# Five edits at the seams of a two-layer hybrid block: rounded-form norm products, an earlier first gather, ln2 folded into x^T, and an alternating split

## The chip, the cores and the metric

The kernel runs on one core of a Trainium2 chip, as one program. The metric is the time of one execution on the device in microseconds. TensorE (PE) multiplies matrices, VectorE (DVE), ScalarE (ACT) and GpSimd (POOL) do the elementwise work, SyncE (SP) starts most of the transfers.

## The reference, cut to what matters

Two layers over 512 tokens of width 1024. Each layer projects x, mixes the tokens in three ways (sparse attention, a gated delta net, a convolution), projects back, normalises, sends each token to 2 of 32 experts, and normalises again.

```python
for l in range(DEPTH):
    h = x @ w_in[l]
    ...
    y_gdn = _gated_deltanet(gdn_qkv, gdn_z, gdn_b, gdn_a, ...)   # q and k are l2-normalised
    mix = jnp.concatenate([y_nsa, y_gdn, y_conf], axis=-1) @ w_out[l]
    x = _layer_norm(DEEPNORM_ALPHA * x + mix, ln1_w[l], ln1_b[l])
    moe = _hier_moe(x, w_group, b_group, w_expert, b_expert, w_gate, w_up, w_down)
    x = _layer_norm(DEEPNORM_ALPHA * x + moe, ln2_w[l], ln2_b[l])
```

All is float32; the products must keep more digits than one rounded-form (F32R) product has.

## The kernel before

Tokens lie in four tiles of 128 (`xr[t]`, t = 0 to 3). TensorE has two ways to multiply float32 here: a full fp32 product, which the trace shows as two records, and the faster product of tiles declared F32R, which holds rounded operands. Where precision matters a value is split into hi (rounded) and lo (the rest), and the products hi·hi, hi·lo and lo·hi are summed (`mm3`, L355 to L357).

A layer goes through these stages. The in-projection transposes x (`xT_ps`, L318), splits it (`xTh`, `xTl`), splits pieces of the weights (`w_hl`, hi by ACT L350, lo by DVE or POOL L351) and fills the PSUM banks `ipA` and `ipB`. In between, the generator `delta_net` and the attention are woven in. `delta_net` makes three rows of inverse norms per head for all tokens (`g_rs`), transposes them (`g_rsT`, L507), and spreads them over the 64 channels of a head by products with a 0/1 selector (`hsel` in the constants; `g_rsb`, L514), six products of a layer; DVE multiplies the six results into q and k. The compression (`cmp_h`) is fp32 too. Then come the out-projection (`opA`, `opB`, `wo_hi`, `wo_lo`), the first normalisation with the router, and the sort of the 32 experts by their load (`r_swp`, `r_sorted`, `r_srt`).

The experts run in nine cycles, largest last ranks sorted into fixed slots of 192 to 32 tokens. SP's queue streams every expert's 6 MB (`w_gu`, `w_d`) through a ring of 13 slots. For a cycle `m_oh` marks which token stands in which slot, `m_ix` are its products, `m_tok` and `m_idx` the token numbers, and POOL gathers the tokens from a DRAM copy of the normalised x (`x1D`) into `xg`; `m_g` transposes, `m_xe` applies the first normalisation's weights, `f_gu` and `f_y` are the two products of the expert, `f_h` the activation, `f_hT` and `f_hTs` its transpose. `y_split` writes an expert's result as hi and lo (`m_yh` by ACT, `m_yl` by DVE); `m_sc` scatters these and DVE adds them to `xr`. The last cycle's results are added in `m_fin`: an fp32 product of `xr` with the identity and four products of `m_yh` and `m_yl` for each tile; statistics, ACT's scale and shift, then `ln_w` and `ln_b` by DVE or POOL follow.

The engines' instruction orders come from a list scheduler at build time; TensorE's order in the expert stage is the program's own (a manual schedule). The lines that a sentence can't say well, the selector product and the split:

```python
T.matmul(ps, C("hsel")[32 * i:32 * i + 4, b * P:(b + 1) * P], rsT[32 * i:32 * i + 4, :],
         start=True, stop=True)
...
for n in range(nj):
    A.copy(hi[:, n * nw:(n + 1) * nw], src[n])
for n in range(nj):
    V.tensor_tensor(lo[:, n * nw:(n + 1) * nw], src[n], hi[:, n * nw:(n + 1) * nw].bitcast(F32), op=ALU.subtract)
```

Of the kernel before, what the change touches and what calls it, by code (L numbers as in the profile page):

```python
# [112 lines left out]
def hybrid_kernel(ctx, tc, x_in, w_in, w_out, cmp_pe, cmp_w1, cmp_w2, conv_w, a_log, dt_bias, norm_w,  # L113
                  dw_w, dw_b, cln_w, cln_b, ln1_w, ln1_b, ln2_w, ln2_b, w_grp, b_grp, w_exp, b_exp,
                  w_gate, w_up, w_down, consts, out, R=3, R2=9, R4=1, NG=10, NE=9, WL=6, layers=DEPTH, CN=32, GI=2, CV0=5, CV1=30, CVM="A", EB=12, SC="GAGA", LB2="GGVVVVVV", TO="0123", HL=3, LOP=4, LOM="10110101", XP=6, ORDER="GkGcomGqPwfx0yG1t2z3GGr"):
# [189 lines left out]
    for l in range(layers):  # L305
        if l:
            mixer, kat, delta, psum = open_mixer(l)

        phase = open_pool(f"inp{l}", "inp")
        xTh, xTl = [], []  # L310
        for kp in range(4):
            a = tp("inp", "xT", 8, f"xTh{kp}", F32R)
            b = tp("inp", "xT", 8, f"xTl{kp}", F32R)
            for kk in range(2):
                k = 2 * kp + kk
                ps = bank("xT_ps")
                for t in range(NT):
# [1333 lines left out]
```

## Time and profile before

| | us |
|---|---|
| timed runs: median of 3 (lowest, highest) | 1934.66 (1930.06, 1935.19) |
| profiled execution | 1942.38 |
| its span in the trace | 1940.6 |
| PE busy in it | 1726.5 (89%) |
| DVE, ACT, POOL busy | 1010.8, 573.2, 390.0 |

The profile is one execution, some 8 us above the median. Its rows give durations and waits; the timed runs give what two kernels are compared by. "Idle before" stands behind an instruction with the event that ended the idle time. The granted clock is TensorE's, 1.00 for its higher level of 2.4 GHz and 0.50 for 1.2 GHz, a mean where a window holds both.

### The profile page before, as it was taken

The page shows a single profiled execution, that of the slowest core. Times are in us where ns is not written, and L with a number is a line of the kernel's source. Part 1 is how long each engine was busy: PE and PEld are TensorE (multiplying, and loading weights), DVE is VectorE, ACT ScalarE, POOL GpSimd, SP SyncE. Part 2 cuts the span into 40 slices and gives each one's busy share as a digit, 9 for nine tenths or more (in the row PEclk, how much of TensorE's full clock was granted, in tenths as well). Part 3 has the DMA queues.
Part 4 walks back from the last instruction along what each step waited for, and adds up shares of the span by engine and source line. Part 5 has one row for each costly group of instructions (what it writes and reads, how often), then busy time and mean ns, then how long its engine had stood idle before and what let it go on. Part 6 is the DMA issues. An engine that isn't in the chain of part 4 may idle for free. (4 is left out here: it accounts for less than half of the span.)

```text
span 1940.6 us, 31342 instructions
## 1 busy us (share of the span) xinstructions
PE 1726.5 (89%) x11812; PEld 1013.2 (52%) x11812; DVE 1010.8 (52%) x2258; ACT 573.2 (30%) x1250; POOL 390.0 (20%) x354
## 2 busy tenths in 40 slices
PE   7899699979889899999789987999698898999996
PEld 6776576763443434333377775767534444343343
DVE  2756877464432524343627678765742334343345
ACT  3342565422210112111234336554221111121122
POOL 2234641324000000000123366323140000000001
PEclk9998699989999899999989975999799998999997
DMA  5221000388999979999632310005799999799994
GB/s 181 88 87 66 1 2 23 130 337 341 408 400 404 404 297 394 409 362 409 250 109 76 99 44 1 13 12 188 285 397 408 403 404 404 282 410 408 363 409 154
DMA packets 147339, 478.41 MB, mean 247 GB/s; under 512 B 23032, under 2 KB 25584, under 8 KB 147184
## 3 DMA queue, kind: packets, MB, share of 16 engines
q1 hardware_dynamic: 138304, 456.74, 61.2%
q10 hardware_dynamic: 4144, 10.70, 1.6%
q0 software_dynamic: 4736, 8.92, 1.3%
q8 instruction: 95, 1.56, 0.3%
q14 instruction: 60, 0.49, 0.1%
HBM read 476.04 MB, written 8.39 MB: 250 GB/s over the span
## 5 line engine op out<-in xcount | busy, mean ns | idle before, releaser
L1291 PE MATMUL f_gu<-w_gu,m_xe 128*32 128x256 f32 (+1 forms) x3456 | 398.0, 453 | 27.4 <-DMA w_gu<-in_moe_w_up 23.2
L1291 PEld LDWEIGHTS f_gu<-w_gu,m_xe 128*32 128x32 f32 (+1 forms) x3456 | 134.7, 118 | 277.8 <-issue 227.7
L1323 PE MATMUL f_y<-w_d,f_hTs 128*32 128x256 f32 (+2 forms) x1824 | 253.0, 474 | 9.3 <-ACT f_hTs L1308 2.9
L1333 DVE TENSOR_TENSOR m_yl<-f_y,m_yh 32x256 fp32r<-32x256 f32 (+2 forms) x222 | 115.3, 520 | 257.9 <-ACT m_yh L1331 250.2
L1383 POOL DMA_INDIRECT xg<-x1D,m_idx x34 | 36.1, 1063 | 753.2 <-PE f_hT L1306 331.9
L1331 ACT CAST m_yh<-f_y 32x256 fp32r<-32x256 f32 (+2 forms) x222 | 98.4, 443 | 299.5 <-PE f_y L1323 297.2
L1444 DVE TENSOR_TENSOR xr<-xr,m_sc 128x1024 f32<-128x1024 f32 x128 | 153.1, 1219 | 26.6 <-PE m_sc L1443 25.4
L1323 PEld LDWEIGHTS f_y<-w_d,f_hTs 128*32 128x32 f32 (+2 forms) x1824 | 82.5, 124 | 157.8 <-issue 127.0
L1298 DVE SCALAR_TENSOR_TENSOR f_h<-f_h,m_wsl,f_gu 128x128 f32<-128x128 f32 (+1 forms) x76 | 33.0, 434 | 229.1 <-ACT f_h L1297 228.7
L1297 ACT ACTIVATE f_h<-f_gu 128x128 f32<-128x128 f32 (+1 forms) x76 | 26.4, 348 | 392.4 <-PE f_gu L1291 298.6
L1443 PE MATMUL m_sc<-m_yh,m_ohT 128*128 128x512 f32 (+1 forms) x256 | 115.4, 451 | 28.9 <-DVE xr L1444 28.6
L351 POOL TENSOR_TENSOR w_hl<-w_slice,w_hl 128x512 fp32r<-128x512 f32 (+1 forms) x54 | 71.9, 1334 | 229.9 <-ACT w_hl L350 220.8
L1443 PE MATMUL m_sc<-m_yl,m_ohT 128*128 128x512 f32 (+1 forms) x256 | 104.7, 409 | 0.0
L350 ACT CAST w_hl<-w_slice 128x512 fp32r<-128x512 f32 (+1 forms) x96 | 56.0, 589 | 145.6 <-PE ipB L357 117.2
L1287 PE MATMUL f_gu<-w_gu,m_xe 128*128 128x512 f32 x192 | 89.1, 610 | 0.4 <-DMA w_gu<-in_moe_w_gate 0.3
L1443 PEld LDWEIGHTS m_sc<-m_yh,m_ohT 128*128 128x128 f32 (+1 forms) x256 | 50.1, 196 | 65.7 <-DVE xr L1444 43.4
L766 POOL TENSOR_TENSOR cvt<-cvt,cv_t 128x485 f32<-128x485 f32 (+28 forms) x66 | 78.3, 1187 | 17.9 <-ACT cv_t L762 16.2
L1028 ACT ACTIVATE e<-a_s,a_nm 128x128 f32<-128x128 f32 (+3 forms) x128 | 66.5, 527 | 44.9 <-DVE a_nm L1023 42.5
L1426 PE MATMUL m_g<-ident,xg 128*128 128x128 f32 (+2 forms) x272 | 47.7, 299 | 19.5 <-DMA xg<-x1D,m_idx 16.2
L1287 PEld LDWEIGHTS f_gu<-w_gu,m_xe 128*128 128x128 f32 x192 | 35.3, 193 | 53.2 <-issue 49.0
L1023 DVE TENSOR_REDUCE a_nm<-a_s 128x1 f32<-128x384 f32 (+3 forms) x88 | 55.3, 635 | 11.9 <-PE a_s L1020 11.0
L351 DVE TENSOR_TENSOR w_hl<-w_slice,w_hl 128x512 fp32r<-128x512 f32 (+1 forms) x42 | 29.3, 697 | 61.8 <-ACT w_hl L350 61.5
(474 smaller groups left out, 3310.0 us busy)
## 6 DMA issues: line engine op xcount, KB each, us to landing
w_gu<-in_moe_w_gate SPq DMA_DIRECT2D x256, 512.0 KB
w_gu<-in_moe_w_up SPq DMA_DIRECT2D x256, 512.0 KB
w_d<-in_moe_w_down SPq DMA_DIRECT2D x128, 1024.0 KB
w_slice<-in_w_in SPq DMA_DIRECT2D x20, 1024.0 KB
w_out<-in_w_out SPq DMA_DIRECT2D x16, 1024.0 KB
x1D<-xr SPq DMA_DIRECT2D x8, 512.0 KB
w_slice<-in_w_in SPq DMA_DIRECT2D x4, 560.0 KB
x<-in_x SPq DMA_DIRECT2D x4, 512.0 KB
```

Of the source, the lines that this page charges most:

```text
L350: A.copy(hi[:, :n], src)
L351: (G if LOE(npc[0], k) else V).tensor_tensor(lo[:, :n], src, hi[:, :n].bitcast(F32), op=ALU.subtract)
L766: G.tensor_tensor(ac2[:, 30 - j:512], ac2[:, 30 - j:512], tm, op=ALU.add)
L1023: V.tensor_reduce(nm[:, 0:hb], ps[:, :hb * L].rearrange("p (h l) -> p h l", h=hb), axis=AX.X, op=ALU.max, negate=True)
L1028: A.activation(e[:, :L], ps[:, i * L:(i + 1) * L], AF.Exp, bias=nm[:, i:i + 1], accum_out=sums[:, i0 + i:i0 + i + 1])
L1287: T.matmul(pg[:, i, :], xe(k), wv[:, i, :], start=(k == 0), stop=(k == 7), skip_group_check=True)
L1291: T.matmul(pg[j * c:(j + 1) * c, 0, 0:2 * fw], xe(k), wv[:, :, j * fw:(j + 1) * fw], start=(k == 0), stop=(k == 7), skip_group_check=True)
L1323: T.matmul(o, lt, wv[:, n * nw:(n + 1) * nw], start=(k == 0), stop=(k == 3), skip_group_check=True)
L1331: A.copy(hi[:, n * nw:(n + 1) * nw], src[n])
L1333: V.tensor_tensor(lo[:, n * nw:(n + 1) * nw], src[n], hi[:, n * nw:(n + 1) * nw].bitcast(F32), op=ALU.subtract)
L1443: T.matmul(ps2[:, n, :], ohT[0:nr, t * P:(t + 1) * P], y[0:nr, n * 512:(n + 1) * 512], start=(i == 0), stop=(i == 1))
L1444: V.tensor_tensor(xr[t][:, :D], xr[t][:, :D], ps2.rearrange("p a b -> p (a b)"), op=ALU.add)
```

## The change

Five edits. (A) The inverse norms are split into hi and lo, put side by side in eight rows, and spread by one F32R product with the selector (`hselr`) instead of an fp32 one. (B) The first cycle's slot marks, token numbers and gather are written ahead of the sort; the DRAM copies of x go by POOL's queue. (C) Between the layers the second normalisation's weights are applied to x^T (channels are rows there, so they are a scale and an offset of ACT's activation), and to the residual later, behind pieces of the in-projection; two of the four `m_fin` tiles leave out the identity product, DVE adds `xr` instead. (D) At the end of the program the scale and shift are four DVE instructions a tile. (E) In `y_split` each copy is followed by its subtract. The path for experts over their slots, not run here, becomes a function. Core of the diff:

```diff
-            V.tensor_scalar(rs3[:, :, 2, 0:4], rn[:, :, 4:8], 0.5, None, op0=ALU.mult)
...
+            rsf, rsh = rs3[:, :, :, 8:12], small("g_rsh", [P, NT, 3, 4], F32R, bufs=1, key="g")
...
+            A.copy(rsh, rsf)
+            V.tensor_tensor(rs3[:, :, :, 4:8], rsf, rsh.bitcast(F32), op=ALU.subtract)
+            V.tensor_copy(rs3[:, :, :, 0:4], rsh.bitcast(F32))
...
-            rsT = s512("g_rsTs")
+            rsT = s512("g_rsTs", F32R)
...
-                    T.matmul(ps, C("hsel")[32 * i:32 * i + 4, b * P:(b + 1) * P], rsT[32 * i:32 * i + 4, :],
+                    T.matmul(ps, hselr[32 * i:32 * i + 8, b * P:(b + 1) * P], rsT[32 * i:32 * i + 8, :],
...
-                nc.sync.dma_start(x1D[l][t * P:(t + 1) * P, :], xr[t][:, :D])
+                G.dma_start(x1D[l][t * P:(t + 1) * P, :], xr[t][:, :D])
...
+        prep_oh(0)
+        ps0 = bank("m_ix0")
+        place_mm(0, ps0, 2, tokb)
+        tokens(0, ps0, 2)
+
         key, keyc = small("r_key", [64, 32], bufs=1), small("r_keyc", [64, 1], bufs=1)
...
             for n in range(nj):
                 A.copy(hi[:, n * nw:(n + 1) * nw], src[n])
-            for n in range(nj):
                 V.tensor_tensor(lo[:, n * nw:(n + 1) * nw], src[n], hi[:, n * nw:(n + 1) * nw].bitcast(F32), op=ALU.subtract)
...
+                    w, o = scale[:, k:k + 1], scale[:, 8 + k:9 + k]
+                    A.activation(hi, ps, AF.Identity, scale=w, bias=o)
+                    xk = xa[:, kk * 512:kk * 512 + 512]
+                    V.tensor_scalar(xk, ps, w, o, op0=ALU.mult, op1=ALU.add)
+                    (G if kk else V).tensor_tensor(lo, xk, hi.bitcast(F32), op=ALU.subtract)
...
+                if later and npc[0] >= 2 and on is V:
+                    for _ in range(2):
+                        f, t = later.popleft()
+                        f(t, made)
...
+        order = (0, 1, 2, 3) if end else (2, 3, 0, 1)
...
+            add = not end and t >= 2
+            if not add:
                 for n in range(2):
+                    T.matmul(fin[t][n], ident, xr[t][:, n * 512:(n + 1) * 512], start=True, stop=False, skip_group_check=True)
+            last_results(t, fin[t], add)
+            if add:
+                V.tensor_tensor(xr[t][:, :D], xr[t][:, :D], f2.rearrange("p a b -> p (a b)"), op=ALU.add)
...
+                if end:
+                    V.scalar_tensor_tensor(o, fin[t][n], mu, lw[:, n * 512:(n + 1) * 512], op0=ALU.subtract, op1=ALU.mult)
+                    V.scalar_tensor_tensor(o, o, rs, lb[:, n * 512:(n + 1) * 512], op0=ALU.mult, op1=ALU.add)
+                else:
+                    A.activation(o, fin[t][n], AF.Identity, scale=rs, bias=nb)
...
+            xTh, xTl = x_transposed(xr, prm[l][:, 124:140])
```

Three places in the engines' orders. The first is TensorE in the in-projection of layer 0, around the transposes of the norms, before:

```order
L355 MATMUL ipB<-xTh_132,w_hl 128x512
L356 MATMUL ipB<-xTl_133,w_hl 128x512
L507 MATMUL g_rsT<-ident,g_rs_1254 96x128 x4
L357 MATMUL ipA<-xTh_132,w_hl 128x512
L355 MATMUL ipA<-xTh_132,w_hl 128x512
```

and of the change, 62 rows later in its order:

```order
L920 MATMUL cmp_h<-kk,w_cmp 128x65 x16
L914 MATMUL cmp_tr<-ident,kva_691 128x128 x2
L914 MATMUL cmp_tr<-ident,kva_692 128x128 x2
L549 MATMUL g_rsT<-ident,g_rs_1262 96x128 x4
L393 MATMUL ipA<-w_hl,xTh_117 128x512
L394 MATMUL ipA<-w_hl,xTh_117 128x512
```

`g_rsT` has moved from the middle of a row of in-projection products to the place behind the compression's transposes. The second place is VectorE after the router in layer 0 (`r_sw` the slot places, `r_key` to `r_pm` the sort of the experts, `m_oh` the slot marks), before:

```order
L1107 TENSOR_TENSOR r_sw_3528<-r_oh_4025,r_oh_4026 128x2x32
L1223 SCALAR_TENSOR_TENSOR r_key<-r_pos,cst 64x32
...
L1361 TENSOR_TENSOR m_oh<-cst,r_sw_3528 128x4x64 x2
L1227 TENSOR_REDUCE r_rank<-r_key 64x1
L1229 TENSOR_SCALAR r_pm<-cst,r_rank 64x64
L1239 COPY r_srt<-r_sorted 128x256
...
L1379 TENSOR_REDUCE m_tok<-m_ix_4202 128x1
...
L1380 TENSOR_SCALAR m_idx<-m_tok 128x1
...
L1246 TENSOR_TENSOR r_tw_4161<-r_rest,r_tw_4161 128x4x2
L1371 TENSOR_SCALAR m_xe_4200<-m_g_4214,w1c_3475,b1c_3476 128x128
```

and of the change:

```order
L1149 TENSOR_TENSOR r_sw_3540<-r_oh_4037,r_oh_4038 128x2x32
L1274 TENSOR_TENSOR m_oh<-cst,r_sw_3540 128x4x64 x2
L1319 SCALAR_TENSOR_TENSOR r_key<-r_pos,cst 64x32
...
L1284 TENSOR_REDUCE m_tok<-m_ix_4150 128x1
L1323 TENSOR_REDUCE r_rank<-r_key 64x1
L1285 TENSOR_SCALAR m_idx<-m_tok 128x1
L1325 TENSOR_SCALAR r_pm<-cst,r_rank 64x64
L1335 COPY r_srt<-r_sorted 128x256
...
L1342 TENSOR_TENSOR r_tw_4192<-r_rest,r_tw_4192 128x4x2
L1438 TENSOR_SCALAR m_xe_4148<-m_g_4226,w1c_3487,b1c_3488 128x128
```

The token numbers (`m_idx`) now stand ahead of the sort's result `r_srt`; the first `m_xe` stands at its old place, behind all of the sort's rows. The third place is ACT and VectorE at an expert of 32 rows, with the engines whose work an instruction waits for; ACT before and of the change:

```order
L1331 CAST m_yh<-f_y 32x256 [waits PE_49]
L1331 CAST m_yh<-f_y 32x256 x3
L1297 ACTIVATE f_h<-f_gu 128x128 [waits PE_49]
```

```order
L1427 CAST m_yh<-f_y 32x256 [waits PE_49]
L1427 CAST m_yh<-f_y 32x256 [waits DVE_49] x3
L1393 ACTIVATE f_h<-f_gu 128x128 [waits PE_49]
```

and VectorE before and of the change:

```order
L1333 TENSOR_TENSOR m_yl<-f_y,m_yh 32x256 [waits Activation_49]
L1333 TENSOR_TENSOR m_yl<-f_y,m_yh 32x256 x3
```

```order
L1428 TENSOR_TENSOR m_yl<-f_y,m_yh 32x256 [waits Activation_49] x4
```

Three of ACT's copies have got a wait for VectorE, and three of VectorE's subtracts one for ACT.

## Rows read from the trace of the kernel before

**Rows 1.** The page: the span and the busy table (busy us, share, instructions of each engine).

```profile
span 1940.6 us, 31342 instructions
PE 1726.5 (89%) x11812; PEld 1013.2 (52%) x11812; DVE 1010.8 (52%) x2258; ACT 573.2 (30%) x1250; POOL 390.0 (20%) x354
```

**Rows 2.** Windows of layer 0's expert stage: the busy us of each engine with its instructions, TensorE's granted clock, the DMA engines' share, and GB/s.

```profile
560.00:680.00 120.00, 102.94 (x628) 49.51 (x624) 47.50 (x108) 18.30 (x44) 4.53 (x4) 0.93 1.03 405
840.00:945.00 105.00, 101.56 (x966) 42.37 (x962) 44.84 (x91) 21.97 (x60) 2.46 (x3) 0.98 0.95 370
```

**Rows 3.** TensorE's waits over the whole program: what it waited for, us in total, times, the longest.

```profile
PE m_g L1426 <- DMA xg<-x1D,m_idx: 16.2, 6, 6.3
PE a_cmp L963 <- DVE qs L957: 11.4, 7, 2.9
```

**Rows 4.** The group of the `g_rsb` products over both layers (busy us, mean ns), and TensorE's timeline of layer 0 with start, duration, shape and count.

```profile
L514 PE MATMUL g_rsb<-g_rsTs,cst 4*128 4x512 f32 x24 | 14.5, 713 | 0.0
138.52 1.98 PE L514 MATMUL g_rsb<-g_rsTs,cst 4*128 4x512 f32 x4
145.33 0.39 PE L357 MATMUL ipA<-w_hl,xTl 128*128 128x512 f32 x1
145.56 0.40 PE L355 MATMUL ipA<-w_hl,xTh 128*128 128x512 f32 x1
149.57 5.10 PE L878 MATMUL cmp_h<-kk,w_cmp 128*128 128x65 f32 x32
154.60 3.78 PE L514 MATMUL g_rsb<-g_rsTs,cst 4*128 4x512 f32 x4
```

**Rows 5.** The group of the `g_rsT` transposes over both layers (the idle time ahead of them last).

```profile
L507 PE MATMUL g_rsT<-ident,g_rs 128*96 128x128 f32 x8 | 1.2, 276 | 3.9 <-DVE g_rs L504 3.9
```

**Rows 6.** Windows around these products, columns as in rows 2.

```profile
118.00:138.00 20.00, 18.03 (x100) 15.32 (x99) 9.73 (x14) 8.88 (x16) 6.85 (x6) 1.00 0.34 106
142.00:145.00 3.00, 3.00 (x9) 2.32 (x8) 2.90 (x6) 0.09 (x1) 0.00 (x0) 0.50 0.19 72
150.00:162.00 12.00, 12.00 (x44) 8.56 (x43) 11.79 (x25) 1.61 (x4) 0.00 (x0) 0.58 0.37 127
```

**Rows 7.** The timelines of ACT, VectorE, TensorE and POOL from the end of layer 0's router to its first expert.

```profile
416.23 2.37 ACT L1160 ACTIVATE xr<-xr,ln_rs 128x1024 f32<-128x1024 f32 x2 [0.50 <-DVE ln_rs L302]
423.61 0.29 DVE L1219 SCALAR_TENSOR_TENSOR r_sw<-r_pos,r_selb 128x128 f32<-128x128 f32 x1
424.85 0.74 DVE L1361 TENSOR_TENSOR m_oh<-cst,r_sw 128x256 bf16<-128x256 f32 x2
428.75 0.26 PE L1391 MATMUL m_ix<-tokb,m_oh 128*128 128x2 bf16 x4
431.10 1.24 POOL L1383 DMA_INDIRECT xg<-x1D,m_idx  x1 [13.91 <-DVE m_idx L1380]
432.87 0.17 DVE L1246 TENSOR_TENSOR r_tw<-r_rest,r_tw 128x8 bf16<-128x8 f32 x1
435.32 1.12 PE L1426 MATMUL m_g<-ident,xg 128*128 128x128 f32 x4 [6.32 <-DMA xg<-x1D,m_idx]
436.05 0.84 DVE L1371 TENSOR_SCALAR m_xe<-m_g,w1c,b1c 128x128 f32<-128x128 f32 x2 [3.02 <-PE m_g L1426]
436.52 1.98 PE L1291 MATMUL f_gu<-w_gu,m_xe 128*64 128x512 f32 x4
```

**Rows 8.** The timelines of ACT and VectorE in the last experts of layer 0.

```profile
859.92 2.70 ACT L1331 CAST m_yh<-f_y 64x512 fp32r<-64x512 f32 x6 [11.35 <-PE f_y L1323]
921.32 2.68 ACT L1331 CAST m_yh<-f_y 64x512 fp32r<-64x512 f32 x6 [6.21 <-PE f_y L1323]
929.41 1.50 ACT L1331 CAST m_yh<-f_y 32x256 fp32r<-32x256 f32 x4 [2.51 <-PE f_y L1323]
930.93 1.73 DVE L1333 TENSOR_TENSOR m_yl<-f_y,m_yh 32x256 fp32r<-32x256 f32 x4 [2.12 <-ACT m_yh L1331]
932.86 0.28 ACT L1297 ACTIVATE f_h<-f_gu 128x128 f32<-128x128 f32 x1 [1.96 <-PE f_gu L1291]
933.17 0.35 DVE L1298 SCALAR_TENSOR_TENSOR f_h<-f_h,m_wsl,f_gu 128x128 f32<-128x128 f32 x1 [0.51 <-ACT f_h L1297]
```

**Rows 9.** The timelines of TensorE and ACT from the end of layer 0 to the first products of layer 1.

```profile
943.18 1.93 PE L1323 MATMUL f_y<-w_d,f_hTs 128*32 128x256 f32 x32
945.18 1.50 ACT L1331 CAST m_yh<-f_y 32x256 fp32r<-32x256 f32 x4 [2.49 <-PE f_y L1323]
948.64 1.95 PE L1598 MATMUL m_fin<-xr,ident 128*128 128x512 f32 x4 [3.52 <-DVEq L1522]
955.26 1.66 ACT L350 CAST w_hl<-w_slice 128x512 fp32r<-128x512 f32 x3 [8.57 <-DMA ln_b<-in_ln_b]
972.23 1.54 PE L318 MATMUL xT_ps<-ident,xr 128*128 128x128 f32 x6 [11.39 <-ACT xr L1610]
976.57 0.80 PE L355 MATMUL ipA<-xTh,w_hl 128*128 128x512 f32 x1 [0.46 <-ACT xTh L250]
```

**Rows 10.** The DMA issues: POOL's load of `m_iot`, count, KB of each, median us from issue to landing.

```profile
m_iot<-consts POOLq DMA_DIRECT2D x2, 256.0 KB, 6.1
```

**Rows 11.** VectorE's timeline at the end of the program: the first statistics and the last add.

```profile
1916.34 1.30 DVE L296 BATCH_NORM_STATS2 ln_st<-m_fin 128x6 f32<-128x512 f32 x2 [6.00 <-PE m_fin L1603]
1935.05 1.23 DVE L1614 TENSOR_TENSOR xr<-xr,ln_b 128x1024 f32<-128x1024 f32 x1
```

More of the change, by code (lines that the diff above doesn't have):

```diff
@@ L205, in load_consts @@
         V.tensor_copy(trib, C("tri_pos"))
+        V.tensor_copy(hselr, C("hsel"))
         V.tensor_copy(tokb, C("tokc").rearrange("p (t c) -> p t c", c=2))
+    hselr = cp.tile([P, 256], F32R, name="hselr")
     tokb = cp.tile([P, NT, 2], BF16, name="tokb")
@@ L305, in hybrid_kernel, with scale_residual, offset_residual @@
     for l in range(layers):
[L306 to L317, printed above, removed]
-                    T.transpose(ps[:, t * P:(t + 1) * P], xs[t][:, k * P:(k + 1) * P], ident)
-                split(a[:, kk * 512:kk * 512 + 512], b[:, kk * 512:kk * 512 + 512], ps)
-            xTh += [a[:, 0:512], a[:, 512:1024]]
-            xTl += [b[:, 0:512], b[:, 512:1024]]
+        if l == 0:
+            xTh, xTl = x_transposed(xs)
+        def scale_residual(t, behind):
+            with tc.issue_after(behind.ins):
+                V.tensor_tensor(xr[t][:, :D], xr[t][:, :D], lw[:, :D], op=ALU.mult)
+        def offset_residual(t, behind):
+            with tc.issue_after(behind.ins):
+                V.tensor_tensor(xr[t][:, :D], xr[t][:, :D], lb[:, :D], op=ALU.add)
+            A.dma_start(x_res[t * P:(t + 1) * P, :], xr[t][:, :D])
+        later = deque((f, t) for t in range(NT) for f in (scale_residual, offset_residual)) if l else deque()
         def load_slice(cuts):
@@ L1587, in hybrid_kernel @@
-        lw, lb = t4("ln_w"), t4("ln_b")
+        overflow()
+        end = l == layers - 1
+        lw, lb = (t4("ln_w"), t4("ln_b")) if end else (x4("ln_w"), x4("ln_b"))
         row_bcast(lw[:, :D], ln2_w[l])
@@ L1611, in hybrid_kernel @@
-        for t in TO:
-            t = int(t)
-            (V if LB2[2 * t] == "V" else G).tensor_tensor(xr[t][:, :D], xr[t][:, :D], lw[:, :D], op=ALU.mult)
-            (V if LB2[2 * t + 1] == "V" else G).tensor_tensor(xr[t][:, :D], xr[t][:, :D], lb[:, :D], op=ALU.add)
-            if l == layers - 1:
+                        T.matmul(o[n], OHT[cy, u][0:nr, t * P:(t + 1) * P], y[0:nr, n * 512:(n + 1) * 512],
+                                 start=first and i == 0 and j == 0, stop=(i == 1 and j == len(last[t]) - 1), skip_group_check=True)
@@ new lines, in hybrid_kernel @@
+        fixed.close()
+        for t in order:
+            mu, rs, nb = norm_stats(fin[t])
+            for n in range(2):
+                o = xr[t][:, n * 512:(n + 1) * 512]
+                if end:
+                    V.scalar_tensor_tensor(o, fin[t][n], mu, lw[:, n * 512:(n + 1) * 512], op0=ALU.subtract, op1=ALU.mult)
+                    V.scalar_tensor_tensor(o, o, rs, lb[:, n * 512:(n + 1) * 512], op0=ALU.mult, op1=ALU.add)
+                else:
+                    A.activation(o, fin[t][n], AF.Identity, scale=rs, bias=nb)
+            if end:
@@ L1622, in hybrid_kernel @@
         close(psum)
-        xs = xr
+        if not end:
+            psum, kat, phase = open_input(l + 1)
+            xTh, xTl = x_transposed(xr, prm[l][:, 124:140])
+            moe.close()
+            mixer, delta = open_mixer(l + 1)
+        else:
+            moe.close()
 _INS = ['x', 'w_in', 'w_out', 'nsa_cmp_pe', 'nsa_cmp_w1', 'nsa_cmp_w2', 'gdn_conv_w', 'gdn_a_log', 'gdn_dt_bias',
```

299 lines of the change are left out of this document (154 added, 145 removed).

## The prediction

> **What bounds the kernel now.** I read the page's busy table and slices first [rows 1]: TensorE works 1726.5 of 1940.6 us, so an edit counts only if it shortens TensorE's own work or one of its waits. The windows show where even that fails [rows 2]: from 560 to 680 us the DMA share is 1.03 and TensorE works 102.9 of 120 us, so the weight stream sets the end there; from 840 to 945 TensorE works 101.6 of 105. The list of TensorE's waits comes next [rows 3]. Most of it lies inside the expert stage; the waits that this change can touch are those for `xg` (16.2 us, longest 6.3), for `g_rs` (3.9, two) [rows 5], and, between the layers, `m_fin`'s 3.52 and `xT_ps`'s 11.39 [rows 9].
>
> **A. The norms' products.** The six `g_rsb` products of a layer are full fp32: 24 records in the two layers, 14.5 us [rows 4]. The row of layer 0 shows four records in 1.98 us, two products, so about one us each. The F32R product of the same 128x512 output starts every 0.23 us beside it at full clock [rows 4] (145.33, then 145.56). After the change all twelve products are of that kind, with eight rows of weights in place of four: 12 x 0.23 = 2.8. Saved 14.5 - 2.8 = 11.7 us. I take the number of weight rows as free, since the 128-row F32R products have that pitch too.
>
> `g_rsT` now stands between `ipB` and `ipA`, and TensorE waits there for `g_rs`, 3.9 us in both layers [rows 5]. In the changed order it stands behind the compression's transposes, some 60 instructions later, where `g_rs` is long made; the wait goes. The additions are an ACT cast, a VectorE subtract and a copy, each of 48 elements a partition, so shorter than the 0.35 us f_h rows of 128 [rows 8]; they lie in the time that `g_rsT` has been moved by. The norms come later by some matmuls, but in the windows of rows 6 TensorE is busy nearly throughout and VectorE is not (15.3 of 20 us): the products set the pace, so I put that at nothing; if the delta net's chain were exposed, the first product's move from 138.5 to about 142 costs 3.5 us a layer, 7 in all. A = 11.7 + 3.9 = 15.6; I take 15.
>
> The clock is a bonus that I leave out of the sum. Behind the fp32 products the granted clock is 0.50 in 142 to 145 and 0.58 in 150 to 162 [rows 6]. If the rise came at once, 3.0 us of work would take 1.5, and of the 12 us, less the 3.8 of `g_rsb` already counted, some 3.4 would go: 5 us in this layer, 10 at most with the other. But the compression's fp32 products (5.10 us, 32 records at 149.57) stay, and they end in the same half-clock stretch [rows 4]. So: between 0 and 10, I take 0.
>
> **B. The moved gather.** Now the first expert's gather stands behind the sort: VectorE writes `r_sw` at 423.61, TensorE does `r_swp`, `r_sorted` and the others before `m_ix` at 428.75, POOL issues the gather at 431.10 and TensorE starts `m_g` at 435.32, after 6.32 us idle [rows 7]. After the change `m_oh` follows `r_sw` directly: 423.61 + 0.29 + 0.3 (`r_sw`'s second half) + 0.74 = 424.9, the placement products 0.3, `m_tok` and `m_idx` behind five short VectorE rows: about 426.2. The gather goes 4.9 us earlier, and with the same 4.2 us from issue to `m_g` its data lie there at 430.6. But the next VectorE row that the expert needs, `m_xe`, still stands behind the whole sort [order of VectorE, above], which ends at 432.87 + 0.17 now, and after the change about 0.7 later, since two `m_oh` (0.74) stand ahead of it. So `m_xe` starts near 433.8, takes 0.42, and `f_gu` starts at 434.3 instead of 436.52: 2.2 us a layer, 4.4 in both. Bounds: 0, if nothing moves, and 9, if `m_xe` came as early as the data. The stream passes it on: its first slot is freed by this expert.
>
> The copies of x for the gather go by POOL's queue instead of SP's. POOL can issue the last when ACT has made it, 416.23 + 2.37 = 418.6 [rows 7], about 419.5 with the others ahead. The nearest row is POOL's `m_iot`: 256 KB in 6.1 us from issue to landing [rows 10]. At that price 425.6, at twice it 431.7; the gather's index is ready at 426.2. I take it as just hidden. A rule speaks against this move: the Trainium skill's page DMA: Bandwidth & Descriptors (section SWDGE vs HWDGE vs iDMA) says that DMAs from GpSimd's queue have their descriptors written by GpSimd's cores, which VectorE can lock out of SBUF in some of its modes, and that queues of SP and ACT are immune. No run here shows such a stall. By it the copies would land late and B would be lost, which is a rival below.
>
> **C. Between the layers.** TensorE ends its last `f_y` at 945.1, waits 3.52 us for the split of `f_y`, needs 12 us for `m_fin`, and waits 11.39 for the normalised, scaled and shifted `xr`; the first `ipA` starts at 976.57 [rows 9]. The change takes the fp32 identity products out of two tiles (1.95 each in the row), puts an add of 1.23 for each on VectorE [rows 11], and moves the eight multiplies and adds of `ln_w` and `ln_b` out of the chain: they come later, under the in-projection. TensorE's `m_fin` then ends near 957. VectorE from 950: two adds and one pair of statistics, 3.7, to 954; then two `w_hl` rows, whose ACT casts start at 955.26, because ACT's queue stands 8.57 us for the landing of `ln_b` [rows 9]: to 957.7 as now. Then three pairs of statistics (1.30 each, rows 11), 3.9, and small rows, to 962.3; ACT's tiles at 1.2 each [rows 7], the last two behind the last statistics, end near 966; transposes (1.0) and the scaled cast (0.6, as `w_hl`'s) bring `ipA` to about 967.6. Gain 9. It would be 12 if the `w_hl` rows did not hold VectorE, and 5 if `ln_b`'s landing came later by the two loads that stand with it.
> The eight moved rows, 8 x 1.23 = 9.8 us, go behind VectorE's pieces in the in-projection, which TensorE bounds; uncovered, they cost up to that much.
>
> **D. The end.** The last tile's add ends at 1935.05 + 1.23 = 1936.28 and the output lands at 1940.6. After the change VectorE does a tile in 1.30 for two statistics over 512, 0.5 for small rows and 4 x 0.65 for the new ones at the same size: 4.4 us. From 1916.34 [rows 11] four tiles end at 1934.0, with two short waits for `m_fin` near 1935. Gain 1.3, between 0 and 2.
>
> **E. The split of `f_y`.** Copy and subtract now alternate, and each waits for the other engine [order of ACT and VectorE, above]. Today four copies take 1.50 us and four subtracts 1.73 behind them [rows 8]: in series already. Alternating adds seven hand-overs; one takes 0.05 (932.86 + 0.28 = 933.14, next row at 933.17). 0.35 more for each 32-row expert. It is exposed ahead of `m_fin`, twice. ACT is free for the next `f_h` by then, as it comes 3.45 us after the split's start. Where six parts of two experts run together (three times, 859.92 to 921.32) `f_h` follows them at once, 0.4 each by the same hand-overs. 2 x (0.4 + 1.2) = 3.2; I take 3. Bounds 0 and, at one us for each of the eight splits from 859.92 to 945.18 [rows 8, 9] in each layer, 16.
>
> **Sum.** 15 + 4.4 + 9 + 1.3 - 3 = 26.7. The profiled execution took 1942.4, above the three timed runs (median 1934.7); so its profile should read 1915.7, and the median 1908.
>
> **Rivals.**
> *The clock follows* (A gives 8 more): 1900. For it, the low clock stands right behind the fp32 products; against it, the compression's products stay.
> *The norms are a chain* (the delta net gives 7 of TensorE's gain back, by the bound under A): 1915. For it, TensorE's 11.4 us of waits for `qs` show chains behind the in-projection [rows 3].
> *`ln_b` holds the boundary* (C gives 5 instead of 9, since two more small loads stand in that queue): 1912. The row of 955.26 speaks for it [rows 9].
> *POOL's copies are late*: the gather stands for them until 431, B is gone: 1912.4.
> *The same mechanism, far worse*: if the copies, issued at 419.5, land beyond 444.5, the first `f_gu` slips over 13.4 us behind today's in each layer and the change is slower, 1936 or more. One step decides it, a landing 25 us after issue, four times `m_iot`'s.
> *The waits of the split are paid often* (8 late experts a layer at 0.8 us in place of 3 in all): 13 instead of 3, 1918.
>
> **Chances.** Forecast 0.47, clock 0.14, norms' chain 0.12, boundary 0.07, copies late 0.07, split 0.07, slow copies 0.03, several losses together 0.03. Range 1897 to 1924: below it lies a clock gain with more of C, above it two of the losses together. A measurement tells 0.3% (6 us) from no change; faster is 0.92, same 0.05, slower 0.03.
>
> **What would show it.** A: `g_rsb` near 0.25 us a record and no wait before `g_rsT`; the clock in 140 to 160 tells the first rival. B: POOL's gather about 5 us ahead, `f_gu` only 2 us, with `m_xe` as what is waited for; if the gather waits for a DMA, the copies are late. C: the first `ipA` about 24.5 us after the last `f_y`'s start instead of 33.4 (943.18 to 976.57). D: the add's row is gone and VectorE runs without a gap. E: the span from the first copy to `m_fin` is 3.8 us instead of 3.5. Wrong it would be if `m_fin`'s or the delta net's waits grow by what the products save.

## The result and the profile after

The changed kernel takes **1910.24 us** (median, 1907.17 to 1913.2) against 1934.93 (1930.06 to 1938.69) for the kernel before: a ratio of 0.9854, 95% interval 0.9813 to 0.9895. The forecast was 1908, the range 1897 to 1924. Two more measurements of the same kernel gave 0.9887 and 0.9839. The profiled execution took 1907.17 us with this span:

```profile
span 1905.4 us, 31305 instructions
PE 1709.5 (90%) x11794; PEld 1004.8 (53%) x11794; DVE 1021.5 (54%) x2281; ACT 569.4 (30%) x1248; POOL 390.7 (21%) x362
```

Against [rows 1] TensorE works 17.0 us less and the span is 35.2 us shorter. The span overstates the gain: the execution profiled before lay 8 us above its median, this one 3 below. To see where the time went, I cut each profile at the same marks of TensorE's timeline, both layers added (us): the in-projection from the first `ipA` to the last `ipB` or `ipA` (the norms' products lie in it); the mixers from there to the last `opB`, the output projection's last product; the routing from there to the first `f_gu`; the experts from there to the end of the last `f_y`; the boundary from there to layer 1's first `ipA`; and the tail from layer 1's last `f_y` to the end.

| kernel | in-proj. | mixers | routing | experts | routing + experts | boundary | tail | span |
|---|---|---|---|---|---|---|---|---|
| before | 327.2 | 467.5 | 51.05 | 1016.8 | 1067.9 | 31.46 | 33.6 | 1940.6 |
| norms_alone | 309.0 | 473.2 | 50.91 | 1013.0 | 1063.9 | 31.33 | 29.7 | 1919.9 |
| **after** | 309.6 | 466.8 | 46.00 | 1019.2 | 1065.2 | 23.85 | 27.4 | 1905.4 |
| after_again | 309.3 | 466.7 | 45.99 | 1022.0 | 1068.0 | 24.32 | 31.6 | 1912.9 |
| after_third | 310.3 | 469.6 | 46.00 | 1021.3 | 1067.3 | 24.69 | 30.6 | 1915.3 |
| f32r_4rows | 311.3 | 474.0 | 46.01 | 1018.6 | 1064.6 | 23.98 | 31.8 | 1918.4 |
| fp32_8rows | 320.3 | 476.3 | 46.02 | 1016.9 | 1062.9 | 23.60 | 29.5 | 1925.2 |
| x1D_sp | 311.1 | 468.3 | 46.00 | 1018.3 | 1064.3 | 24.44 | 28.9 | 1910.0 |
| xe_early | 311.1 | 466.8 | 44.21 | 1022.0 | 1066.2 | 23.96 | 29.0 | 1909.9 |
| split_undone | 310.3 | 469.2 | 46.02 | 1019.7 | 1065.7 | 21.38 | 27.2 | 1906.6 |
| ln_sp | 310.4 | 468.2 | 46.00 | 1022.0 | 1068.0 | 22.88 | 30.9 | 1913.5 |
| best | 309.5 | 472.1 | 43.51 | 1022.3 | 1065.8 | 20.84 | 31.5 | 1912.4 |
| ids_late | 309.2 | 468.1 | 46.01 | 1007.8 | 1053.8 | 24.92 | 29.1 | 1897.7 |
| ids_split | 310.5 | 474.4 | 46.00 | 1011.2 | 1057.2 | 21.31 | 28.8 | 1904.9 |

The three profiles of the unchanged new kernel show how far a column may be trusted: routing within 0.01, boundary and in-projection within 1, mixers and experts within 3, tail within some 4 us (over all rows with the same mixers, 466.7 to 474.4). So the gain stands in the in-projection (-17.6, -17.9 and -16.9), at the boundary (-6.8 to -7.6), in the tail (-2.0 to -6.2), and in the routing (-5.05). But the experts grow by what the routing gains: routing and experts together are 1065.2 to 1068.0 after, and 1067.9 and 1063.9 in the two kernels with the old routing.

**The norms.** The group of `g_rsb`, [rows 4] before, and TensorE's timeline of layer 0 after the change (start, duration, count):

```profile
L556 PE MATMUL g_rsb<-g_rsTs,hselr 8*128 8x512 f32 x12 | 4.9, 462 | 0.0
137.40 0.60 PE L549 MATMUL g_rsT<-ident,g_rs 128*96 128x128 f32 x4
142.93 0.73 PE L556 MATMUL g_rsb<-g_rsTs,hselr 8*128 8x512 f32 x2
145.77 3.79 PE L920 MATMUL cmp_h<-kk,w_cmp 128*128 128x65 f32 x32
```

24 records of 14.5 us became 12 of 4.9; `g_rsT` waits for nothing, and the compression's second `cmp_h`, 5.10 us before, takes 3.79. The windows of that stretch (columns as in [rows 2]: behind the window's length TensorE, its weight loads, VectorE, ACT and POOL, then the granted clock, the DMA share and GB/s):

```profile
140.00:150.00 10.00, 10.00 (x59) 8.12 (x57) 9.70 (x14) 1.73 (x3) 1.29 (x1) 1.00 0.46 166
150.00:160.00 10.00, 10.00 (x42) 7.32 (x42) 9.96 (x20) 3.04 (x7) 4.40 (x3) 1.00 0.30 106
```

The granted clock is at its upper level (2.4 GHz) throughout, where [rows 6] had 0.50 in 142 to 145 and 0.58 in 150 to 162.

**The routing.** Timelines of POOL, VectorE and TensorE in layer 0:

```profile
409.73 0.54 POOL L1203 DMA_DIRECT2D x1D<-xr  x1 [0.54 <-ACT xr L1202]
416.56 0.14 DVE L1285 TENSOR_SCALAR m_idx<-m_tok 128x1 int32<-128x1 f32 x1
418.63 1.09 POOL L1288 DMA_INDIRECT xg<-x1D,m_idx  x1 [7.83 <-DMA x1D<-xr]
422.11 1.12 PE L1472 MATMUL m_g<-ident,xg 128*128 128x128 f32 x4 [1.66 <-DMA xg<-x1D,m_idx]
424.34 0.72 DVE L1438 TENSOR_SCALAR m_xe<-m_g,w1c,b1c 128x128 f32<-128x128 f32 x2
424.80 1.97 PE L1387 MATMUL f_gu<-w_gu,m_xe 128*64 128x512 f32 x4 [1.57 <-DVE m_xe L1438]
```

The index is ready at 416.70, but the gather leaves at 418.63: POOL waits 1.9 us more for the landing of the last copy of x, 8.9 us after its issue. `m_xe` stands behind the sort, as expected, and `f_gu` waits for that.

**The boundary.** TensorE and ACT between the layers; compare [rows 9]:

```profile
931.24 1.93 PE L1419 MATMUL f_y<-w_d,f_hTs 128*32 128x256 f32 x32
937.52 0.52 PE L1641 MATMUL m_fin<-m_yh,m_ohT 64*128 64x512 f32 x1 [4.35 <-DVEq L1520]
937.85 0.62 PE L1641 MATMUL m_fin<-m_yl,m_ohT 64*128 64x512 f32 x1
940.96 3.78 PE L1653 MATMUL m_fin<-xr,ident 128*128 128x512 f32 x4
943.72 1.66 ACT L383 CAST w_hl<-w_slice 128x512 fp32r<-128x512 f32 x3 [7.58 <-DMA ln_w<-in_ln_w]
954.99 1.97 PE L152 MATMUL xT_ps<-ident,xr 128*128 128x128 f32 x8 [6.08 <-ACT xr L1667]
957.02 0.80 PE L393 MATMUL ipA<-xTh,w_hl 128*128 128x512 f32 x1
```

The wait for `xr` fell from 11.39 to 6.08. The wait ahead of `m_fin` grew from 3.52 to 4.35, and behind it the products run at half clock: 0.62 us each, and 3.78 for four identity products that take 1.95 in [rows 9]. Whether the boundary pays for that is asked in experiment 5.

### The profile page after: what moved, and what is told of

Same layout as the page of the kernel before. It is cut to its first block, busy times and chain, and to the rows that moved or that the text cites. A ratio compares the mean times of both kernels' runs of the same rounds, so it can differ in the third digit from the quotient of the medians.

```text
span 1905.4 us, 31305 instructions
## 1 busy us (share of the span) xinstructions
PE 1709.5 (90%) x11794; PEld 1004.8 (53%) x11794; DVE 1021.5 (54%) x2281; ACT 569.4 (30%) x1248; POOL 390.7 (21%) x362
## 5 line engine op out<-in xcount | busy, mean ns | idle before, releaser
L1419 PE MATMUL f_y<-w_d,f_hTs 128*32 128x256 f32 (+2 forms) x1824 | 257.0, 478 | 10.1 <-ACT f_hTs L1404 2.9
L1383 PEld LDWEIGHTS f_gu<-w_gu,m_xe 128*128 128x128 f32 x192 | 35.2, 193 | 52.9 <-issue 47.2
L1065 DVE TENSOR_REDUCE a_nm<-a_s 128x1 f32<-128x384 f32 (+3 forms) x88 | 55.5, 636 | 12.8 <-PE a_s L1062 11.7
L1436 ACT ACTIVATE m_xe<-m_g,b1c,w1c 128x256 f32<-128x256 f32 (+3 forms) x72 | 37.0, 541 | 72.3 <-DVE m_xe L1438 72.2
```

Source lines behind the costliest of these rows:

```text
L1065: V.tensor_reduce(nm[:, 0:hb], ps[:, :hb * L].rearrange("p (h l) -> p h l", h=hb), axis=AX.X, op=ALU.max, negate=True)
L1383: T.matmul(pg[:, i, :], xe(k), wv[:, i, :], start=(k == 0), stop=(k == 7), skip_group_check=True)
L1419: T.matmul(o, lt, wv[:, n * nw:(n + 1) * nw], start=(k == 0), stop=(k == 3), skip_group_check=True)
```

## The experiments

All ratios are to the kernel before, measured beside the run. What the expectations call the router's last product is the last `opB` of the table's marks.

**1. norms_alone: the kernel before with edit A only** (the rounded-form products of two exact parts, and their constant).

```
+rsf, rsh = rs3[:, :, :, 8:12], small("g_rsh", [P, NT, 3, 4], F32R, bufs=1, key="g")
+A.copy(rsh, rsf)
+V.tensor_tensor(rs3[:, :, :, 4:8], rsf, rsh.bitcast(F32), op=ALU.subtract)
+V.tensor_copy(rs3[:, :, :, 0:4], rsh.bitcast(F32))
-T.matmul(ps, C("hsel")[32 * i:32 * i + 4, b * P:(b + 1) * P], rsT[32 * i:32 * i + 4, :],
+T.matmul(ps, hselr[32 * i:32 * i + 8, b * P:(b + 1) * P], rsT[32 * i:32 * i + 8, :],
```

> The kernel before with edit A alone. Theory 'products, wait and clock': the in-projection of layer 0 ends about 10 us earlier than before at a granted clock of 1.00 from 140 to 160 us, some 3 us are given back before the out-projection, layer 1 gives 7 to 12; together 15 to 19 us. Rival 'products and wait only' (the clock of the changed kernel comes from other edits): the clock falls to 0.5 to 0.6 again and the gain is 12 to 15. Rival 'norms' chain': most of it is given back, the gain is under 9.

1919.33 us, 0.9892 (0.984 to 0.9943). The in-projection is as short as in the whole change, -18.2, and the other stages differ from before's by up to 5.7 us either way, as they do among kernels with the same code there. The norms alone give most of the gain.

**2. fp32_8rows and f32r_4rows: the form and the number of rows apart.** The first keeps everything of the change but makes the same eight-row products in full fp32; the second keeps the rounded form and multiplies the first part only, with four rows (the second part is left out).

```
-    hselr = cp.tile([P, 256], F32R, name="hselr")
+    hselr = cp.tile([P, 256], F32, name="hselr")
-            rsT = s512("g_rsTs", F32R)
+            rsT = s512("g_rsTs")
```

> The changed kernel with the twelve products as full fp32 products of the same eight rows, all else as it is. By the records, 12 us more of TensorE time. If it is the fp32 products that pull the granted clock down, it falls to 0.5 to 0.6 in 140 to 160 us again, and the kernel is 15 to 20 us slower than the changed one. If it was that they had four rows only, the clock stays at 1.00 and the loss is near 12 or less.

> The changed kernel with four rows (the hi part only; the lo part of the norms is left out of the products). If the form is what counts: same time as the changed kernel within 0.3%, g_rsb rows unchanged, clock 1.00 from 140 to 160. If the number of rows counts for the clock, it falls behind these products and 4 to 8 us are lost.

Full fp32: 1934.61 us, 0.9981 (0.9955 to 1.0006). Rounded, four rows: 1912.41, 0.9853 (0.9799 to 0.9907); the unchanged new kernel measured beside them, after_again, 1917.37, 0.9887 (0.9836 to 0.9939).

> The changed kernel unchanged, for a second trace of it: how far the stages of two executions of the same program lie apart. Expected: each stage within 1 us, except those where the clock falls at a wait (the m_fin products at the end of a layer), 3 to 4 us.

The group of fp32_8rows, two windows and TensorE's timeline at the second one, then the group of f32r_4rows:

```profile
L556 PE MATMUL g_rsb<-g_rsTs,hselr 8*128 8x512 f32 x24 | 13.4, 668 | 0.0
140.00:150.00 10.00, 10.00 (x55) 7.67 (x55) 9.73 (x14) 1.72 (x3) 1.29 (x1) 1.00 0.45 163
150.00:160.00 10.00, 10.00 (x31) 6.28 (x30) 9.93 (x18) 1.75 (x4) 3.25 (x2) 0.83 0.31 106
146.50 3.79 PE L920 MATMUL cmp_h<-kk,w_cmp 128*128 128x65 f32 x32
150.22 1.98 PE L556 MATMUL g_rsb<-g_rsTs,hselr 8*128 8x512 f32 x4
152.75 0.63 PE L394 MATMUL ipB<-w_hl,xTh 128*128 128x512 f32 x1
```

```profile
L556 PE MATMUL g_rsb<-g_rsTs,hselr 4*128 4x512 f32 x12 | 4.9, 462 | 0.0
```

Rows are free: four or eight take 4.9 us. The form is what counts: 13.4 against 4.9, and with fp32 the clock falls to 0.83 in a window in which TensorE works 10.00 of 10.00 us. It is 1.00 from 140 to 150, although four fp32 records stand there too (142.87 to 144.85), and 0.50 from 152.62 on, 0.4 us behind the next four. Those follow `cmp_h` directly, the first four stand 5 us behind theirs. The kernel before agrees: its clock is at 0.50 for 20.5 us at four places in the two layers (from 141.56, 151.80, 1104.12 and 1121.19), and each begins inside, or at most 1.1 us behind, a stretch in which `cmp_h` and fp32 `g_rsb` records follow each other. The wait at `g_rsT` isn't the cause: it ends at 121.17, and the clock is 1.00 through it, from 118 to 138 [rows 6]. So the falls go with the fp32 form right behind the compression, of which the changed order leaves fewer places; no run here sets these products apart from `cmp_h` and changes nothing else. The in-projection is 10.7 us longer than after's, 8.5 of them the products themselves. Against before, fp32_8rows still saves 6.9 there: 3.9 are the wait at `g_rsT`, 1.1 the group, and most of the rest the second `cmp_h`, which takes 3.79 here too. The times differ by 17 us from after_again's; what goes beyond the 10.7 lies mostly in the mixers of one profile (476.3) and isn't explained.

**3. x1D_sp: the copies of x from SP's queue.**

```
-                G.dma_start(x1D[l][t * P:(t + 1) * P, :], xr[t][:, :D])
+                nc.sync.dma_start(x1D[l][t * P:(t + 1) * P, :], xr[t][:, :D])
```

> The changed kernel with the copies of x issued by SP's queue as before. Theory 'the copies are late, but m_xe is what counts': POOL's gather no longer stands for a landing and comes about 2 us earlier, m_g follows it 2 us earlier, and the first f_gu stays within 0.5 us, since m_xe is still behind the sort on VectorE; from the last opB to f_gu 22.5 to 23 us. Rival 'the copies' landing is what counts': f_gu comes 1.5 to 2 us earlier in each layer.

1914.16 us, 0.9833 (0.9777 to 0.9889). SP's issue of the last two copies, POOL's gather and TensorE's first `f_gu`:

```profile
407.11 1.46 SPq L1203 DMA_DIRECT2D x1D<-xr  x2
418.15 1.11 POOL L1288 DMA_INDIRECT xg<-x1D,m_idx  x1 [11.34 <-DMA x1D<-xr]
423.60 1.98 PE L1387 MATMUL f_gu<-w_gu,m_xe 128*64 128x512 f32 x4 [0.82 <-DVE m_xe L1438]
```

The gather still waits for the copies, and leaves 17.6 us behind the last `opB` (400.6), not sooner than from POOL (16.8). Routing is 46.00 as before the edit. The 2 us that were expected of the gather didn't come, and the late landing isn't a matter of POOL's queue.

**4. xe_early: with that, the first chunk's gather and `m_xe` ahead of the slot tables** on VectorE.

```
+        for kp in range(GI):
+            gather(0, kp)
+        xm = XM[0]
-        parts3(tw[:, :, 2:98], srt[:, :, 1, :], 32)
+        with tc.issue_after(xm.ins):
+            parts3(tw[:, :, 2:98], srt[:, :, 1, :], 32)
```

> As the run with the copies on SP's queue, and the rest of the sort (the weights' three parts, the overflow count, the next cycle's slot marks) ordered behind the first m_xe on VectorE. If m_xe behind the sort is what the moved gather still waits for: from the last opB to f_gu about 20 us instead of 23 in each layer, 5 to 6 us in all, unless the next cycle's marks, now later, make TensorE wait at m_ws or m_ix for what was saved. Rival: the wait only moves there, and the gain is under 1.

1910.25 us, 0.9831 (0.977 to 0.9892). TensorE in layer 0:

```profile
421.75 1.12 PE L1338 MATMUL m_g<-ident,xg 128*128 128x128 f32 x4 [2.68 <-DMA xg<-x1D,m_idx]
422.94 1.97 PE L1419 MATMUL f_gu<-w_gu,m_xe 128*64 128x512 f32 x4
```

`f_gu` follows `m_g` at once now, but `m_g` waits for the gathered rows, which wait for the copies: routing gains 0.5 and 1.3 us where 3 a layer were expected. Nor do routing and experts together become shorter (1066.2).

**5. split_undone: the split as copies, then subtracts,** as before the change.

```
             for n in range(nj):
                 A.copy(hi[:, n * nw:(n + 1) * nw], src[n])
+            for n in range(nj):
                 V.tensor_tensor(lo[...], src[n], hi[...].bitcast(F32), op=ALU.subtract)
```

> The changed kernel with all copies of the split ahead of all subtracts, as before. Theory 'seven hand-overs': TensorE's wait for m_fin goes back from 4.35 and 3.81 to 3.5, the expert stage loses 1 us a layer, 2 to 3 us in all. Rival 'paid often': 10 us. Rival 'free': under 0.5.

1908.41 us, 0.9812 (0.9762 to 0.9862). TensorE at the boundary:

```profile
937.50 0.47 PE L1642 MATMUL m_fin<-m_yh,m_ohT 64*128 64x512 f32 x1 [3.52 <-DVEq L1521]
937.81 0.39 PE L1642 MATMUL m_fin<-m_yl,m_ohT 64*128 64x512 f32 x1
```

The wait is 3.52 again, the first products have the full clock (0.39 each, where after has 0.62), and the boundary is 21.38 in place of 23.85. Routing and experts stay where they were: no cost of the alternation shows among the late experts.

Is it the clock that makes a wait longer by 0.83 us cost 2.5? The windows around the start of `m_fin`, of after, of split_undone, and of ids_split (experiment 8), which has the split undone too:

```profile
936.00:948.00 12.00, 10.48 (x21) 5.07 (x22) 7.45 (x12) 1.80 (x4) 1.76 (x2) 0.72 0.82 287
```

```profile
936.00:948.00 12.00, 9.79 (x24) 4.57 (x24) 8.68 (x17) 2.00 (x4) 2.22 (x2) 0.86 0.91 310
```

```profile
939.00:951.00 12.00, 10.14 (x21) 5.05 (x21) 8.73 (x18) 1.72 (x4) 2.23 (x2) 0.72 0.91 314
```

ids_split has after's clock, 0.72, with its `m_fin` products at 0.63 each, and its boundary is 21.31 all the same. So it isn't the clock: TensorE waits for `xr` afterwards anyway, and that chain runs on ACT and VectorE. Their rows follow, behind a register load of VectorE's queue (its ns, then its start in us); first of after, where ACT's casts of `w_hl` start at 943.72, 10.55 us behind the last `f_y`:

```profile
L1519 DVEq TENSOR_LOAD <-r_novi x1: 543/543/543, 936.2 to 936.2; - x1
944.37 0.69 DVE L385 TENSOR_TENSOR w_hl<-w_slice,w_hl 128x512 fp32r<-128x512 f32 x1 [1.23 <-ACT w_hl L383]
945.41 1.36 DVE L385 TENSOR_TENSOR w_hl<-w_slice,w_hl 128x512 fp32r<-128x512 f32 x1 [0.35 <-ACT w_hl L383]
946.70 0.68 DVE L330 BATCH_NORM_STATS2 ln_st<-xr 128x6 f32<-128x512 f32 x1
```

and of split_undone, where they start 9.71 us behind the last `f_y` (which ends at 933.98):

```profile
L1520 DVEq TENSOR_LOAD <-r_novi x1: 545/545/545, 935.6 to 935.6; - x1
935.58 1.72 DVE L1429 TENSOR_TENSOR m_yl<-f_y,m_yh 32x256 fp32r<-32x256 f32 x4 [2.11 <-ACTq L1521]
943.69 1.66 ACT L383 CAST w_hl<-w_slice 128x512 fp32r<-128x512 f32 x3 [8.14 <-DMA ln_b<-in_ln_b]
944.34 0.69 DVE L385 TENSOR_TENSOR w_hl<-w_slice,w_hl 128x512 fp32r<-128x512 f32 x1 [1.86 <-ACT w_hl L383]
944.95 1.28 DVE L330 BATCH_NORM_STATS2 ln_st<-xr 128x6 f32<-128x512 f32 x2
946.20 0.68 DVE L385 TENSOR_TENSOR w_hl<-w_slice,w_hl 128x512 fp32r<-128x512 f32 x1
```

Three things differ. The alternating split ends only 0.11 us later (3.43 us behind the last `f_y` instead of 3.32); the other 0.7 of the wait goes with VectorE's load of a register (`r_novi`, the count for the path of experts over their slots) and the branch on it, which ran under the four subtracts and now start with the last of them. ACT's queue issues the loads of `ln_w` and `ln_b`, for whose landing the casts stand, behind its last copies, at 3.55 and 4.36 us instead of 1.81 and 3.53: the casts start 0.84 us later. And VectorE does both `w_hl` subtracts ahead of the second tile's statistics instead of one behind them. From ACT's first cast to the first `ipA` it is 13.3 us in the three profiles of the new kernel and in ids_late, and 11.66 in split_undone and ids_split. So 0.84 and 1.6 make up the 2.5. That VectorE's order is the 1.6 is read from these rows; no run changes it alone.

**6. ln_sp: the next layer's `ln_w` and `ln_b` from SP's queue,** to test whether they hold the `w_hl` casts.

```
+        rb = row_bcast if end else row_bcast_s
-        row_bcast(lw[:, :D], ln2_w[l])
+        rb(lw[:, :D], ln2_w[l])
```

> The changed kernel with ln2's two rows loaded by SP's queue at the end of layer 0, so that ACT's queue does not stand for their landing ahead of the w_hl casts. If VectorE's chain is held by these casts alone: the first ipA of layer 1 comes 3 us earlier after the last f_y (20.8 instead of 23.9). If the two fp32 m_fin tiles are the next bound: 1.0 to 1.6 us. Rival: nothing, since ACT's statistics-bound tiles end last anyway.

1911.45 us, 0.9817 (0.9768 to 0.9867). The ACT cast behind the end of the layer:

```profile
950.21 1.66 ACT L383 CAST w_hl<-w_slice 128x512 fp32r<-128x512 f32 x3 [10.87 <-DMA w_slice<-in_w_in]
```

ACT now stands there for the weights, which SP loads behind the two rows: the casts start 13.84 us behind the last `f_y`, where the new kernel's three profiles have 10.55 to 11.41. The boundary is 22.88 even so, 1 to 1.8 under these three, as VectorE does both tiles' statistics of `xr` ahead of `w_hl`. The edit moves the wait and the order, and so doesn't price the landing of the rows by itself.

**7. best: edits 3 to 6 together, beside after_third, the new kernel once more.**

> The changed kernel with four edits together: the 512 KB row copies issued by SP, the first chunk's gather ahead of the slot tables, the split as copies then subtracts, and the next layer's normalisation rows on SP's queue. If the gains read in the single runs add up: route 22.5 and 21.7 us in place of 23.0 (1.8 together), boundary 21.4 less about 1 (20 to 21 in place of 23.9), last wait of m_fin 3.53 in place of 4.35 and 3.8, so 5 to 6 us, the ratio to the unchanged changed kernel of the same call 0.997. If the landing of the normalisation rows and the split share one wait, the boundary stays at 21.4 and the sum is 4. If the gains lie within what the clock moves from execution to execution (the stage between the first projections and the router differs by 8 us and more between runs of unlike kernels), the two intervals overlap.

> The changed kernel itself, for comparison in the same call: ratio 0.985 to 0.989 to the kernel before; route 23.0 us in each layer, boundary 23.9 to 24.3 and m_fin's last wait 4.35 in layer 0, 3.8 in layer 1.

1913.81 us, 0.9858 (0.9819 to 0.9896), against 1911.14, 0.9839 (0.9808 to 0.9869). The single gains add up where they were read (routing 43.51, boundary 20.84), and the kernel isn't faster: routing and experts together are 1065.8 again. So the 2.5 us of the routing don't arrive, and the 3.0 to 3.9 of the boundary are less than what mixers and tail move by.

**8. ids_late and ids_split: who gives the routing's gain back.** In the table the experts take back every gain of the routing. Counted from the last `opB`, the first three groups of `f_y` in layer 0 end at 40.2, 53.4 and 66.7 us after the change and at 42.7, 56.0 and 69.2 before; the seventh ends at 117.4 to 119.4 in the two layers of the new kernel's three profiles, and at 117.1 to 119.1 in those of before and norms_alone. In between the lead is lost to the weight stream. SP's weight loads, first of the kernel before (last `opB` at 410.97), then of the new one (401.81):

```profile
429.67 0.37 SPq L1191 DMA_DIRECT2D w_gu<-in_moe_w_gate  x1
441.64 0.34 SPq L1191 DMA_DIRECT2D w_gu<-in_moe_w_gate  x1
```

```profile
SPq L1611 <- DVE r_lv L1360: 17.8, 1, 17.8
421.82 0.34 SPq L1233 DMA_DIRECT2D w_gu<-in_moe_w_up  x1
433.11 0.01 SPq L1233 DMA_DIRECT2D w_gu<-in_moe_w_gate  x1
```

SP stands 17.8 us for the sort, since the experts behind the first two are named by it, loads one pair, and the next only 11.3 us later. Its order explains that: 18 register loads of experts' numbers stand between the two pairs.

```
84 L1233 DMA w_gu<-in_moe_w_gate 128x1024 [waits DMAHW0_49]
85 L1233 ISA
86 L1233 DMA w_gu<-in_moe_w_up 128x1024 [waits DMAHW1_49]
87 L1611 TENSOR_LOAD r_id
88 L1611 ISA x2
89 L1611 TENSOR_LOAD r_id
```

Measured from the last `opB`, the first weight load behind this pair leaves at 30.7 us before and 31.3 after: the change moved the gather, not the sort. The edit loads each number only behind the weights of the expert before it (and `r_novi` behind those of the first expert so named; not shown):

```
-                    ev = nc.values_load(ids[0:1, r:r + 1], ...)
+                    with tc.issue_after(LAST[0].ins):
+                        ev = nc.values_load(ids[0:1, r:r + 1], ...)
```

> The changed kernel, with each sorted expert's number loaded into SP's registers only behind the weight loads of the expert before it; in the changed kernel 18 of these loads stand in one row behind the first two weight loads, between 421.82 and 433.11 us. Counted from the router's last product, SP's first weight loads are at 20.0 and the next at 31.4 us in the changed kernel and at 19.2 to 19.4 and 31.2 to 31.4 in the kernel before, although the first f_gu starts 2.5 us earlier after the change; and router's last product to last f_y takes 531 to 535 us a layer in both. If the stream of weights sets the end of the experts and its restart stands behind these register loads, the second pair goes out when its slot is free, near 28 us, and the 531 to 535 us become 528 to 532, 6 us in the two layers, a ratio to the kernel before of 0.981 to 0.984. If the stream is not what gives the 2.5 us back, the loads go out earlier and the 531 to 535 us stay.

> The same, with the split as four copies and then four subtracts. Boundary 21.4 us in place of 23.9 and the last waits of m_fin 3.53, as with that edit alone; the experts' stage as in the run with only the loads moved. If both hold, 9 us under the changed kernel and a ratio of 0.980; if the loads move nothing, 3 us and 0.983.

ids_late 1908.22 us, 0.9829 (0.9792 to 0.9866); ids_split 1906.6, 0.9819 (0.9781 to 0.9857). SP in ids_late, whose last `opB` starts at 398.51:

```profile
418.53 0.34 SPq L1235 DMA_DIRECT2D w_gu<-in_moe_w_up  x1
426.44 0.33 SPq L1235 DMA_DIRECT2D w_gu<-in_moe_w_gate  x1
```

The load behind the pair leaves at 27.9 us, when its slot's last product ends. The seventh group of `f_y` ends at 114.4 to 116.1 in the two kernels' layers, some 3 us sooner than in the new kernel, and routing and experts take 1053.8 and 1057.2 us in the two layers: below all twelve other profiles (1062.9 to 1068.0), by 5.7 us and more. So it is the restart of the weight stream behind the sort, and not the gather moved ahead of it, that the experts' end follows. The two lie 10.3 us under the mean of those with the whole change (1065.8); the earlier restart, 3.4 a layer, accounts for 6.8. The edit spreads the later number loads too; whether the other 3.5 come from them stays open. By time the two are 2 to 4 us under the new kernel's first median, and the intervals of the ratios overlap.

## Why the prediction came out right, and where it was lucky

**The sum** was 26.7 us; the medians differ by 24.7. Term by term the table gives nearly the same sum in other parts.

**A, 15.** The mechanism held; two sizes were off and nearly cancel. The products went from 14.5 to 4.9, a gain of 9.6 in place of 11.7: I took 0.23 us each, the pitch of F32R products in a row, and here they come singly or in pairs, 0.73 us a pair. The wait of 3.9 went. The rest of the stage's 17.6, about 4, goes with the clock, taken as 0 within 0 to 10: the rival that the clock follows came true in part. Its counterargument, that the compression's fp32 products stay, was wrong: they run at full clock now, 3.79 us. What goes with the falls is the fp32 form of `g_rsb` right behind the compression (experiment 2). One reading under A was wrong: the 15.3 of 20 us that the prediction gives as VectorE's [rows 6] are TensorE's weight loads. VectorE has 9.73 there, but 2.90 of 3.00 and 11.79 of 12.00 in the two windows around the products, so it was nearly as busy as TensorE, and the ground for putting the chain at nothing was missing. That it held was luck: after the change TensorE works 10.00 of 10.00 us in both windows shown. The rival of a chain in the delta net, 7 back, isn't seen: the mixers average 469.5 over the eleven rows with the whole change and F32R products, before's one profile has 467.5; 2 us of it can't be told.

**B, 4.4.** The first `f_gu` came 2.5 us sooner a layer, for 2.2 forecast, with `m_xe` behind the sort as what it waits for (426.2 and 4.2 are 430.4 there, not 430.6; nothing hangs on it). Two steps were wrong. The first is "I take it as just hidden": the copies took 8.9 us, not `m_iot`'s 6.1, and landed 1.9 us late; it cost nothing, as `m_xe` came later still. And the rule of the Trainium skill's page DMA: Bandwidth & Descriptors (section SWDGE vs HWDGE vs iDMA), which I had weighed against POOL's queue, doesn't explain it: the copies from SP's queue landed no sooner (experiment 3). The second, which lost the term, is "The stream passes it on: its first slot is freed by this expert": SP's first loads stand for the sort's numbers, and then behind 18 register loads. B is worth about nothing at the end, within the 3 to 4 us by which routing and experts move. The rival of a far later landing needed 25 us; it was 8.9.

**C and E, 9 and -3.** With the split undone the boundary is 21.3 to 21.4, 10.1 under before's 31.46: C is 10, within 5 to 12. No run undoes C or D alone; their sizes are read from the stages in which they lie, and norms_alone, which has neither, keeps before's boundary (31.33). `ln_b`'s rival, 4 us, isn't seen: ACT's casts start 9.64 to 9.71 us behind the last `f_y` there, 10.15 before. E was right in size by luck. I had 0.4 a layer ahead of `m_fin` for hand-overs and 1.2 among the late experts. The hand-overs cost 0.11, and nothing shows among the late experts, where the rival of often paid waits had put 13. The wait did grow, by 0.8 and 0.3, but mostly through a register load, and the 2.5 at the boundary come through ACT's casts and VectorE's order (experiment 5), neither of which I had; the 0.3 is the wait at the program's end.

**D, 1.3.** From TensorE's last product to the end it is 11.4 us in place of 13.4, so 2.0. What else the tail shows (27.4 to 31.6 after, 33.6 before) is the clock of `m_fin` in single executions.

Together 17.5 + 0 + 10.1 - 2.8 + 2.0 = 26.8, as forecast: B's 4.4 was lost, and the clock (4, less 2.1 at the products), C and D made it good. That the total came out within 2 us is luck as far as these sizes go.

## What to carry to other kernels

A gain ahead of a stream counts only if it also starts the stream sooner: look for what the loads' own queue waits for, register loads included, before passing a gain on. Small full-fp32 products can cost twice, in their own time and in the clock of the work behind them. And when a small edit costs more than its own wait, look at what else it moved before blaming the clock: here the place of a register load, the issue of two transfers and another engine's order, shown by a run with the same half clock and without the cost.
